# Two ways of turning the input of a superblock, and a wider gap between its load and its norm

## The chip, the cores and the metric

One core of one Trainium2 chip runs the whole kernel. The metric is the device time of one execution in microseconds (us), as the median of several runs. The profile is of one execution, which has a time of its own.

## The reference, cut to what matters

One decoder layer over a sequence of 4096 tokens of width 1024, with fp32 inputs:

```python
h = rmsnorm(x, norm_g) * (1.0 + scale) + shift      # scale, shift, gate: from c @ w_ada
proj = h @ w_in                                     # 1024 -> 3328 columns: q, k, v, gate of two head groups
y_sb = stick_breaking_attention(q, k, v) * silu(g)  # 8 heads of 64
y_sw = sliding_window_sink_attention(...) * silu(g) # 8 query heads, 2 key heads, window 128
x = x + gate * (concat(y_sb, y_sw) @ w_out)
out = rmsnorm(x, final_g)
```

Tokens are on the partitions in x; the projections need h with its 1024 features on the partitions, so every block of 128 tokens has to be turned. Each fp32 operand of a product is split into an fp16 upper half and an fp16 remainder, and a product is three passes on TensorE.

## The kernel before, in words

The sequence is cut into eight superblocks s = 0..7 of 512 tokens (`T`), each of four blocks of 128 (`NB`). `main` (L684) writes the whole order of the work into one list, `fill`, of small items with a planned cost each, and runs it from the front to the end. A superblock has 26 **units**, numbered 0 to 25 (`step`, L738): unit 0 is the key chunk of the window group, 1 to 3 three gate chunks, 4 the first query chunk; then the value units, further query and gate chunks (5 to 13); then, four times, a key, a query and a gate chunk of the stick-breaking group (14 to 25). In superblocks 1 to 7, units 5 to 9 are value units, unit 10 is the second query chunk, and behind units 10, 12 and 13 stand the output products (`o_items`, L655) of the superblock before. A chunk unit is four items of six matmuls (`part`, L398), planned at 1300 ns an item, and ends with its evacuation by ScalarE and VectorE. A query chunk's evacuation is followed by two small copies `q<-q` across partitions (L431) issued from ScalarE's queue, and the scores (`att_s1`, L516, L519, L523) need them.

Attention goes by ticks. Each pair of heads makes two groups; a group has its scores and softmax (`att_s1`), the split of its weights into two halves (`split_w`, L589, L590), the turning of these halves by DMA (`att_s2`, L595, on SyncE's queue) and the product with the values (`att_s3`, L608). A tick's due time is the planned time at the end of the pair's query unit plus `LAG` (8000 ns for the window group) plus a multiple of `TICK` (5200 ns). Ticks are written in front of the first item that is not earlier than their due time; `later(n, ...)` puts a piece of work n items later. Each engine, and each queue of DMAs, works strictly in the order written.

The input of superblock s + 1 is made ready during superblock s by `x_items` (L349), four steps for each block b: `load` (x from HBM, L318, SyncE's queue; for block 0 also the two rows of scale and shift, broadcast to all partitions, L305 and L306), `norm` (square and sum on ScalarE, L325; reciprocal root on GpSimd, L312 and L313; two items later the modulation, VectorE L365 and GpSimd L366), `split` (upper half on ScalarE L372, remainder on GpSimd L373) and `turn` (two transposing DMAs, L379). A step is placed behind the unit that `when` gives it (L731, L732):

```python
            o, e = (0, 4) if s else (9, 3)
            when = [[o + i + 3 * b for b in range(NB)] for i in (0, 1, 2, e)]
```

So for s of 1 to 6 the loads stand behind units 0, 3, 6, 9, the norms behind 1, 4, 7, 10, the splits behind 2, 5, 8, 11 and the turns behind 4, 7, 10, 13. In superblock 0 all of it stands nine units later, from 9 to 21. Superblock 7 has none of it.

Superblock 0's own input is turned at the start by fp32 transposes on TensorE (`setup_x0`, L146, L171 and L172). During superblock 0 the weights are also staged: each chunk unit loads one chunk of `w_in` (L273), splits one on ScalarE (L289) and VectorE (L290), and writes it to a scratch in HBM (L293). And `setup_wo_items` (L217) prepares the output weights in items that are strewn in by a count of the items written (`beat`, L714 to L721): every fourth one (every second one near the start). Those are eight loads, eight `gates`, then `bcast` (L239, L242, VectorE), `spread` (two fp32 products on TensorE, L247, which need bcast's result, and their evacuation) and eight `wo` (VectorE L254, ScalarE L260, GpSimd L261). Steps of `x_items` count as items too.

The tiles `f` (four buffers, in turn) hold x, the staged weights and the output rows; `hi` and `bc` have two buffers, the PSUM tiles `mm` four and `z` one.

Of the kernel before, what the change touches and what calls it, by code (L numbers as in the profile page):

```python
# [7 lines left out]
F32 = mybir.dt.float32  # L8
F16 = mybir.dt.float16
# [3 lines left out]
AF = mybir.ActivationFunctionType  # L13
ALU = mybir.AluOpType
# [3 lines left out]
D = 1024  # L18
KD = D // 128
# [3 lines left out]
T = 512  # L23
NB = T // 128
# [28 lines left out]
class Kern:  # L53
# [163 lines left out]
    def setup_wo_items(self):  # L217

        nc = self.nc
        pool = self.P["yT"].pool  # L220
        half = lambda i, name: pool.tile([128, 512], F32, tag=f"yT{i}", name=name)
        gb = [half(8 + n, "gb") for n in range(2)]
        raw = self.wo.rearrange("p m e n -> p m (e n)").bitcast(F32)
        st = {}

        def gates(k):
            ck = self.cond[:, k:k + 1]
            for n in range(2):
                t = raw[:, k, n * 512:(n + 1) * 512]
                if k == 0:  # L230
                    nc.vector.tensor_scalar(out=gb[n], in0=t, scalar1=ck, scalar2=None, op0=ALU.mult)
                else:
                    nc.vector.scalar_tensor_tensor(out=gb[n], in0=t, scalar=ck, in1=gb[n], op0=ALU.mult, op1=ALU.add)
            self.later(4, lambda: nc.sync.dma_start(out=raw[:, k], in_=self.w_out[k * 128:(k + 1) * 128, :]))

        def bcast():
            for k in range(KD):
                sl = gb[k // 4][:, (k % 4) * 128:(k % 4 + 1) * 128]
                nc.vector.scalar_tensor_tensor(out=sl, in0=self.ident, scalar=self.col[:, 32 + k:33 + k], in1=sl,  # L239
                                               op0=ALU.mult, op1=ALU.add)  # L240
            ones = st["ones"] = half(10, "onesq")[:, 0:128]
            nc.vector.memset(ones, 1.0)  # L242

        def spread():
            pss = [self.mm(), self.mm()]
            for n in range(2):
                nc.tensor.matmul(out=pss[n], lhsT=st["ones"], rhs=gb[n], start=True, stop=True)  # L247
            for n in range(2):
                nc.vector.tensor_scalar(out=gb[n], in0=pss[n], scalar1=WS, scalar2=None, op0=ALU.mult)

        def wo(m):
            t = [half(10 + n, "wot") for n in range(2)]
            for n in range(2):
                nc.vector.tensor_tensor(out=t[n], in0=raw[:, m, n * 512:(n + 1) * 512], in1=gb[n], op=ALU.mult)  # L254
            self.later(2, lambda: halves(t, m))

        def halves(t, m):
            for n in range(2):
                sl = slice(n * 512, (n + 1) * 512)
                nc.scalar.activation(self.wo[:, m, 0, sl], t[n], AF.Copy)  # L260
                nc.gpsimd.tensor_tensor(out=self.wo[:, m, 1, sl], in0=t[n], in1=self.wo[:, m, 0, sl], op=ALU.subtract)  # L261

        return [lambda k=k: self.mod_load(2, k, raw[:, k]) for k in range(KD)] + \
            [lambda k=k: gates(k) for k in range(KD)] + [bcast, spread] + [lambda m=m: wo(m) for m in range(KD)]


    def stage_load(self):
# [81 lines left out]
    def x_items(self, s, row0):  # L349

        nc = self.nc
        st = {}

        def load(b):
            if b == 0:
                self.load_mod()
            st[b] = self.x_load(self.x[bass.ds(row0 + b * 128, 128), :])

        def norm(b):
            xt = st[b]  # L360
            r = self.ssq(xt, self.hT[s][:, b, 0])
            self.later(2, lambda: modulate(xt, r))

        def modulate(xt, r):
            nc.vector.scalar_tensor_tensor(out=xt, in0=xt, scalar=r, in1=self.ab, op0=ALU.mult, op1=ALU.mult)  # L365
            nc.gpsimd.tensor_tensor(out=xt, in0=xt, in1=self.sb, op=ALU.add)  # L366

        def split(b):
            xt = st[b]
            hi = self.P["hi"].tile([128, D], F16, tag="hi", name="hi")  # L370
            lo = xt.bitcast(F16)[:, 0:D]
            nc.scalar.activation(hi, xt, AF.Copy)  # L372
            nc.gpsimd.tensor_tensor(out=lo, in0=xt, in1=hi, op=ALU.subtract)  # L373
            st[b] = (hi, lo)

        def turn(b):
            hl = st.pop(b)
            for e in range(2):
                nc.sync.dma_start_transpose(out=self.hT[s][:, b, e], in_=hl[e])  # L379

        return [[(0.0, lambda f=f, b=b: f(b)) for f in (load, norm, split, turn)] for b in range(NB)]


    def chunk_items(self, s, c, evac):
# [299 lines left out]
    def main(self):  # L684
        nc = self.nc
        NS = self.NS
# [29 lines left out]
        def add(items, after=-1):  # L716
            for ns, f in items:
                fill.append((ns, f, after))
                beat[0] += 1
                if extra and (beat[0] % 4 == 0 or 6 <= beat[0] < 20 and beat[0] % 2 == 0):  # L720
                    fill.append((0.0, extra.pop(0), -1))  # L721

        def pair_groups(s, pair):
            for g in range(2):
                self.groups.append((len(fill), s, pair, g))

        last_group = {}
        for s in range(NS):
            xi = self.x_items(s + 1, (s + 1) * T) if s + 1 < NS else []
            xat = {}  # L730
            o, e = (0, 4) if s else (9, 3)  # L731
            when = [[o + i + 3 * b for b in range(NB)] for i in (0, 1, 2, e)]  # L732
            for b, its in enumerate(xi):
                for i, it in enumerate(its):
                    xat.setdefault(when[i][b], []).append(it)
            unit = [0]

            def step(items, after=-1):  # L738
                add(items, after)
                add(xat.pop(unit[0], []))  # L740
                unit[0] += 1

            add([(0.0, lambda s=s: self.new_hT(s + 1))])
            step(self.chunk_items(s, SWK, self.evac_k(s, 4, "ksw")))
            for p in range(3):
                step(self.chunk_items(s, SWG + p, self.evac_g(s, 4 + p)))
            vi = self.v_items(s, s * NB)
            step(self.chunk_items(s, SWQ, self.evac_q(s, 4)))
            pair_groups(s, 4)
            nv = 5 if s else 3  # L750
            vo = [0, 1, 4, 2, 3]
            for i in vo[:nv]:
                step(vi[i])
            for p in range(1, 4):
                if p == 2:
                    step(self.chunk_items(s, SWG + 3, self.evac_g(s, 7)))
                step(self.chunk_items(s, SWQ + p, self.evac_q(s, 4 + p)))
                pair_groups(s, 4 + p)
                if s > 0 and p == 1:
                    add([(0.0, self.load_fg)])  # L760
                if s > 0:
                    add(self.o_block(s - 1, p - 1, (s - 1) * T), last_group[s - 1])
                elif p < 3:
                    step(vi[vo[2 + p]])
            if s > 0:
                add(self.o_block(s - 1, 3, (s - 1) * T), last_group[s - 1])
            for p in range(4):
                chunks = [self.chunk_items(s, SBK + p, self.evac_k(s, p, "ksb")),
                          self.chunk_items(s, SBQ + p, self.evac_q(s, p)),
                          self.chunk_items(s, SBG + p, self.evac_g(s, p))]  # L770
                for ch in chunks:
                    step(ch)
                pair_groups(s, p)
            assert not extra and not xat, (len(extra), xat)
            last_group[s] = len(self.groups) - 1
# [251 lines left out]
```

## Time and profile before

| | |
|---|---|
| median of 3 runs | 1802.67 us (1802.04 to 1804.15) |
| the profiled execution: its time | 1803.36 us |
| the profiled execution: span from first to last instruction | 1801.7 us |
| mean granted TensorE clock | 0.971 |
| busy: VectorE, ScalarE, GpSimd | 57%, 40%, 33% |
| TensorE's chain: share of matmul line L398 in the chain that ended last | 38% |

A busy TensorE is not one at its peak, since its clock is granted in two levels, 1.2 and 2.4 GHz (0.5 and 1.0 of full speed; a mean between them is a mixture over time). A wait is put down to the semaphore that came last.

### The profile page before, as it was taken

The page shows a single profiled execution, that of the slowest core. Times are in us where ns is not written, and L with a number is a line of the kernel's source. Part 1 is how long each engine was busy: PE and PEld are TensorE (multiplying, and loading weights), DVE is VectorE, ACT ScalarE, POOL GpSimd, SP SyncE. Part 2 cuts the span into 40 slices and gives each one's busy share as a digit, 9 for nine tenths or more (in the row PEclk, how much of TensorE's full clock was granted, in tenths as well). Part 3 has the DMA queues.
Part 4 walks back from the last instruction along what each step waited for, and adds up shares of the span by engine and source line. Part 5 has one row for each costly group of instructions (what it writes and reads, how often), then busy time and mean ns, then how long its engine had stood idle before and what let it go on. Part 6 is the DMA issues. An engine that isn't in the chain of part 4 may idle for free.

```text
span 1801.7 us, 28070 instructions
## 1 busy us (share of the span) xinstructions
PE 1676.5 (93%) x10758; PEld 859.3 (48%) x10758; DVE 1028.4 (57%) x1853; ACT 720.4 (40%) x1416; POOL 592.6 (33%) x737
## 2 busy tenths in 40 slices
PE   3797689999999999999999999999999999999987
PEld 2353334454554555544554545545555445545443
DVE  6468786455745656554654557456564556345562
ACT  3345543354334433444334534344434434244331
POOL 2015644332344323432343323343243323123231
PEclk9898889999999999999999999999999999999999
DMA  7877688475765677557674767557575567445552
GB/s 269 285 216 166 138 213 189 112 161 146 166 151 147 149 156 185 109 149 170 148 194 100 166 154 177 138 141 163 149 182 120 148 163 156 107 123 131 152 135 72
DMA packets 425859, 283.52 MB, mean 157 GB/s; under 512 B 350156, under 2 KB 376820, under 8 KB 425716
## 3 DMA queue, kind: packets, MB, share of 16 engines
q1 hardware_dynamic: 383428, 185.16, 45.2%
q10 hardware_dynamic: 42288, 96.49, 18.2%
q8 instruction: 86, 1.41, 0.3%
q14 instruction: 57, 0.47, 0.1%
HBM read 152.59 MB, written 27.80 MB: 100 GB/s over the span
## 4 chain that ended last, share of the span: by engine, by line
PE 72%; DVE 8%; DMA 6%; POOL 4%; ACT 4%; issue 3%; SPq 1%; ACTq 0%; POOLq 0%; DVEq 0%
PE mm L398 38%; PE mm L655 16%; PE mm L471 6%; PE pv L608 5%; PE z L523 4%; DMA f<-in_x_dram 3%; PE mm L483 2%; DMA q<-q 2%; ACT p L567 1%; POOL p L576 1%; DVE acc L127 1%; POOL f L366 1%; DVE w L290 1%; DMA f<-in_w_in_dram 1%; PE z L519 1%
## 5 line engine op out<-in xcount | busy, mean ns | idle before, releaser
L398 PE MATMUL mm<-hT,w 128*128 128x512 f16 x4032 | 918.9, 384 | 16.9 <-DVE w L290 8.6
L398 PEld LDWEIGHTS <-w 128*128 128x128 f16 x4032 | 389.9, 99 | 477.3 <-issue 23.4
L655 PE MATMUL mm<-wo,yT 128*128 128x512 f16 x1536 | 353.3, 386 | 0.0
L576 POOL TENSOR_SCALAR p<-p,smm 128x256 f32<-128x256 f32 x256 | 122.2, 498 | 419.6 <-DVE smm L574 360.0
L655 PEld LDWEIGHTS <-yT 128*128 128x128 f16 x1536 | 150.5, 99 | 175.8 <-issue 8.8
L626 POOL TENSOR_TENSOR yT<-gs,yT 128x256 f16<-128x256 f32 x128 | 140.0, 1093 | 240.5 <-DVE yT L625 223.2
L567 ACT ACTIVATE p<-sp,nm 128x256 f32<-128x256 f32 (+1 forms) x256 | 126.0, 493 | 204.2 <-DVE nm L560 204.0
L471 PE MATMUL mm<-wv,hT 128*128 128x512 f16 x768 | 175.2, 383 | 6.2 <-ACT wv L289 5.5
L537 DVE TENSOR_TENSOR_SCAN nb<-nb,d 128x768 f32<-128x768 f32 x64 | 115.9, 1810 | 112.1 <-ACT nb L531 112.1
L533 POOL TENSOR_SCALAR_AFFINE_SELECT beta<-beta 128x512 f32<-128x512 f32 x64 | 83.7, 1308 | 257.9 <-ACT beta L532 214.2
L590 DVE SCALAR_TENSOR_TENSOR w<-p,w 128x1024 f16<-128x1024 f32 x64 | 85.1, 1330 | 68.8 <-ACT w L589 68.8
L589 ACT ACTIVATE w<-beta 128x768 f16<-128x768 f32 x64 | 53.9, 843 | 165.4 <-DMA wT<-w 95.9
L471 PEld LDWEIGHTS <-hT 128*128 128x128 f16 x768 | 74.9, 99 | 93.0 <-issue 9.8
L560 DVE CUSTOM_DVE_ANT_0 sp<-z,bias,nsink 128x256 f32<-128x256 f32 (+1 forms) x256 | 107.2, 474 | 14.8 <-PE z L523 14.4
L608 PEld LDWEIGHTS <-v 128*64 128x64 f16 x2304 | 89.1, 110 | 55.4 <-issue 51.4
L608 PE MATMUL pv<-wT,v 128*64 128x128 f16 (+1 forms) x2304 | 110.1, 240 | 3.5 <-DVE yT L625 2.5
L531 ACT ACTIVATE nb<-z 128x768 f32<-128x768 f32 x64 | 51.7, 808 | 134.4 <-issue 58.5
L589 ACT ACTIVATE w<-p 128x1024 f16<-128x1024 f32 x64 | 67.6, 1056 | 86.8 <-POOL p L576 37.6
L366 POOL TENSOR_TENSOR f<-f,sb 128x1024 f32<-128x1024 f32 x28 | 75.5, 2695 | 44.9 <-DVE f L365 44.9
L462 DVE SCALAR_TENSOR_TENSOR v<-mm,v 128x512 f16<-128x512 f32 (+1 forms) x64 | 31.3, 489 | 94.0 <-ACT v L461 92.5
L373 POOL TENSOR_TENSOR f<-f,hi 128x1024 f16<-128x1024 f32 x28 | 61.4, 2194 | 63.5 <-ACT hi L372 63.5
L590 DVE SCALAR_TENSOR_TENSOR w<-beta,w 128x768 f16<-128x768 f32 x64 | 62.4, 976 | 34.7 <-ACT w L589 34.7
(108 smaller groups left out, 1700.6 us busy)
## 6 DMA issues: line engine op xcount, KB each, us to landing
w<-wsc ACTq DMA_DIRECT2D x147, 512.0 KB, 3.5
f<-in_x_dram SPq DMA_DIRECT2D x64, 512.0 KB, 4.2
q<-q ACTq DMA_DIRECT2D x128, 128.0 KB, 3.6
out_dram<-f SPq DMA_DIRECT2D x32, 512.0 KB, 3.9
f<-in_w_in_dram SPq DMA_DIRECT2D x26, 512.0 KB, 6.8
wo<-in_w_ada_dram SPq DMA_DIRECT2D x24, 512.0 KB, 8.1
wsc<-w SPq DMA_DIRECT2D x21, 512.0 KB, 5.1
wo<-in_w_out_dram SPq DMA_DIRECT2D x8, 512.0 KB, 5.5
```

The source lines that it names most:

```text
L366: nc.gpsimd.tensor_tensor(out=xt, in0=xt, in1=self.sb, op=ALU.add)
L398: nc.tensor.matmul(out=ps, lhsT=w[:, k, a, :], rhs=hT[:, :, b, k, :], start=(k == 0 and i == 0), stop=(k == KD - 1 and i == 2))
L471: nc.tensor.matmul(out=ps, lhsT=hT[:, tb, b, k, :], rhs=self.wv[:, k, a, 0:512], start=(k == 0 and i == 0), stop=(k == KD - 1 and i == 2))
L537: nc.vector.tensor_tensor_scan(out=nbf, data0=nbf, data1=d1, initial=1.0, op0=ALU.mult, op1=ALU.max)
L560: nc.vector.tensor_tensor_reduce(out=sp[:, u, c0:256], in0=z[:, u, c0:256], in1=bias[:, c0:256], scale=-2.0 ** -(h + 1), scalar=self.nsink ...
L567: nc.scalar.activation(p[:, u, c0:256], sp[:, u, c0:256], AF.Exp, scale=-1.0, bias=nm[:, u:u + 1], accum_out=sm[:, u:u + 1])
L576: nc.gpsimd.tensor_scalar(out=p[:, u, :], in0=p[:, u, :], scalar1=sm[:, u:u + 1], scalar2=1.0, op0=ALU.mult, op1=ALU.mult)
L589: nc.scalar.activation(hi, w, AF.Copy, scale=WS)
L590: nc.vector.scalar_tensor_tensor(out=lo, in0=w, scalar=WS, in1=hi, op0=ALU.mult, op1=ALU.subtract)
L608: nc.tensor.matmul(out=pv[h * 64:(h + 1) * 64, o0:o0 + c1 - c0], lhsT=v[:, a, vc:vc + 64], rhs=wT[:, e, h, c0:c1], start=(n == 0 and i == ...
L626: nc.gpsimd.tensor_tensor(out=y[:, 1, cols], in0=y32, in1=y[:, 0, cols], op=ALU.subtract)
L655: nc.tensor.matmul(out=ps, lhsT=y[:, a, tb * 128:(tb + 1) * 128], rhs=self.wo[:, m, b, n * 512:(n + 1) * 512], start=(m == OORD[0] and i = ...
```

## The change

Three edits. The input of superblock 1 is made ready by a new function, `x_items_pe`, on two pairs of blocks: load, norm without modulation (L328, in place), then for every two of the eight column groups of 128 four fp32 transposes on TensorE into one PSUM tile, two ScalarE passes that apply scale and shift from columns (tile `h32`, in the buffers `hi`), and for each of the two blocks a VectorE copy to fp16 and a GpSimd subtraction. Its steps stand behind units 19 to 25. For superblocks 2 to 7 the four steps stay as they are, and their places change. An empty item is put between `bcast` and `spread`.

```diff
-            [lambda k=k: gates(k) for k in range(KD)] + [bcast, spread] + [lambda m=m: wo(m) for m in range(KD)]
+            [lambda k=k: gates(k) for k in range(KD)] + [bcast, lambda: None, spread] + [lambda m=m: wo(m) for m in range(KD)]
...
+    def x_items_pe(self, s, row0):
...
+        def load(g):
+            for b in (2 * g, 2 * g + 1):
+                st[b] = self.x_load(self.x[bass.ds(row0 + b * 128, 128), :])
+
+        def norm(g):
+            for b in (2 * g, 2 * g + 1):
+                self.x_norm(st[b], self.hT[s][:, b, 0])
+
+        def tr(g, k):
+            ps = self.mm()
+            for j in range(2):
+                for i in range(2):
+                    nc.tensor.transpose(ps[:, j * 256 + i * 128: j * 256 + (i + 1) * 128],
+                                        st[2 * g + i][:, (k + j) * 128:(k + j + 1) * 128], self.ident)
+            h = self.P["hi"].tile([128, D], F16, tag="hi", name="h32").bitcast(F32).rearrange("p (j n) -> p j n", j=2)
+            for j in range(2):
+                nc.scalar.activation(h[:, j, :], ps[:, j * 256:(j + 1) * 256], AF.Identity,
+                                     bias=self.s16[:, k + j:k + j + 1], scale=self.a16[:, k + j:k + j + 1])
+            for i in range(2):
+                hT = self.hT[s][:, 2 * g + i]
+                hb = h[:, :, i * 128:(i + 1) * 128]
+                nc.vector.tensor_copy(hT[:, 0, k:k + 2, :], hb)
+                nc.gpsimd.tensor_tensor(out=hT[:, 1, k:k + 2, :], in0=hb, in1=hT[:, 0, k:k + 2, :], op=ALU.subtract)
+
+        return [[(0.0, lambda g=g: load(g)), (0.0, lambda g=g: norm(g))] +
+                [(440.0, lambda g=g, k=k: tr(g, k)) for k in range(0, KD, 2)] for g in range(2)]
...
-            xi = self.x_items(s + 1, (s + 1) * T) if s + 1 < NS else []
+            xi = [] if s + 1 == NS else (self.x_items if s else self.x_items_pe)(s + 1, (s + 1) * T)
             xat = {}
-            o, e = (0, 4) if s else (9, 3)
-            when = [[o + i + 3 * b for b in range(NB)] for i in (0, 1, 2, e)]
+            when = [[0, 2, 5, 8], [2, 4, 7, 10], [3, 5, 8, 11], [5, 7, 10, 13]]
+            if s == 0:
+                when = [[19, 22], [20, 23], [21, 24], [21, 24], [22, 25], [22, 25]]
```

For s of 1 to 6 block 0 is loaded behind the same unit and normed, split and turned one unit later; blocks 1 to 3 are loaded one unit earlier (2, 5, 8 for 3, 6, 9), and their other steps stay.

## Rows read from the trace of the kernel before

**Rows 1.** The page, part 1: busy time, share of the span, instructions.

```profile
PE 1676.5 (93%) x10758; PEld 859.3 (48%) x10758; DVE 1028.4 (57%) x1853; ACT 720.4 (40%) x1416; POOL 592.6 (33%) x737
```

**Rows 2.** Windows: superblocks 0, 1 to 6, 7, cut at unit 25's evacuation (L445).

```profile
core 0: us, PE busy (x) PEld busy (x) DVE busy (x) ACT busy (x) POOL busy (x), PEclk, DMA share, GB/s
56.00:276.31 220.31, 171.31 (x1018) 83.90 (x1016) 154.02 (x250) 104.60 (x193) 85.91 (x91) 0.88 0.77 208
276.31:1529.67 1253.36, 1227.13 (x7992) 629.31 (x7992) 704.09 (x1309) 509.19 (x1022) 431.25 (x529) 0.99 0.65 153
1529.67:1732.55 202.88, 202.88 (x1338) 104.54 (x1338) 108.67 (x216) 76.89 (x159) 49.90 (x73) 1.00 0.53 130
```

**Rows 3.** Windows: 20 us around unit 10 of superblocks 1, 6, 7; superblock 1's unit 3.

```profile
345.00:365.00 20.00, 15.86 (x89) 7.46 (x87) 6.43 (x17) 4.47 (x13) 5.12 (x8) 0.91 0.57 143
1392.00:1412.00 20.00, 16.12 (x90) 7.94 (x89) 6.25 (x16) 6.46 (x15) 5.67 (x9) 0.91 0.60 162
1597.00:1617.00 20.00, 20.00 (x120) 10.14 (x119) 7.69 (x22) 6.26 (x14) 4.12 (x7) 1.00 0.60 168
300.00:320.00 20.00, 18.46 (x140) 10.55 (x139) 8.18 (x10) 4.71 (x7) 8.74 (x8) 1.00 0.66 145
```

**Rows 4.** Timeline, superblock 2, units 8 to 10: start, length, engine, [idle before <-releaser].

```profile
538.86 16.04 SPq L595 DMA_TRANSPOSE wT<-w  x4
...
554.95 0.57 SPq L318 DMA_DIRECT2D f<-in_x_dram  x1
554.99 0.69 DVE L416 SCALAR_TENSOR_TENSOR q<-mm,q 64x512 f16<-64x512 f32 x1
...
559.16 1.06 ACT L325 ACTIVATE hT<-f 128x1024 bf16<-128x1024 f32 x1 [6.05 <-DMA f<-in_x_dram]
559.17 1.13 ACTq L431 DMA_DIRECT2D q<-q  x2
...
562.23 0.26 PE L516 MATMUL z<-kp,q 128*128 128x128 f16 x1 [3.99 <-DMA q<-q]
```

**Rows 5.** Timeline of superblock 7, unit 10, ScalarE's queue and TensorE.

```profile
1596.40 1.21 ACTq L431 DMA_DIRECT2D q<-q  x2
...
1603.22 0.27 PE L516 MATMUL z<-kp,q 128*128 128x128 f16 x2
```

**Rows 6.** Waits of TensorE from 115 to 290 us: total, times, longest.

```profile
PE z L516 <- DVE nm L560: 11.2, 2, 7.0
PE mm L398 <- DVE w L290: 8.4, 3, 6.6
PE mm L247 <- DVE onesq L242: 7.5, 1, 7.5
```

**Rows 7.** Waits of ScalarE from 115 to 280 us.

```profile
ACT hi L372 <- POOL f L366: 8.6, 3, 4.2
...
ACT hT L325 <- DMA f<-in_x_dram: 3.9, 1, 3.9
```

**Rows 8.** Window of 120 us inside superblock 0 (columns as in rows 2).

```profile
140.00:260.00 120.00, 86.08 (x502) 41.47 (x503) 93.86 (x151) 61.49 (x116) 70.55 (x69) 0.85 0.68 162
```

**Rows 9.** Groups by line: busy us, mean ns of one | idle before.

```profile
L626 POOL TENSOR_TENSOR yT<-gs,yT 128x256 f16<-128x256 f32 x128 | 140.0, 1093 | 240.5 <-DVE yT L625 223.2 <-DMA wT<-w 15.1 <-PE mm L655 2.1
...
L625 DVE CAST yT<-gs 128x256 f16<-128x256 f32 x128 | 51.6, 403 | 4.4
...
L171 PE MATMUL mm<-ident,f 128*128 128x128 f32 x32 | 5.1, 337 | 0.0
...
L172 ACT ACTIVATE xT<-mm,a 128x512 f32<-128x512 f32 x8 | 5.0, 690 | 6.3 <-PE mm L171 6.3
```

**Rows 10.** Window of the start's 32 fp32 transposes (columns as in rows 2).

```profile
26.80:32.00 5.20, 5.17 (x33) 4.93 (x33) 4.82 (x7) 3.71 (x7) 0.00 (x0) 1.00 0.61 244
```

**Rows 11.** The page, part 6: the input's transposing DMAs and their landing.

```profile
hT<-hi SPq DMA_TRANSPOSE x28, 4.5
```

**Rows 12.** Timeline at 136 us: a GpSimd addition and a VectorE cast side by side.

```profile
136.43 2.34 POOL L366 TENSOR_TENSOR f<-f,sb 128x1024 f32<-128x1024 f32 x1 [3.94 <-DVE f L365]
136.66 2.26 DVE L625 CAST yT<-gs 128x256 f16<-128x256 f32 x1
```

More of the change, by code (lines that the diff above doesn't have):

```diff
@@ L381, in x_items @@
         return [[(0.0, lambda f=f, b=b: f(b)) for f in (load, norm, split, turn)] for b in range(NB)]
+    def x_items_pe(self, s, row0):
+        nc = self.nc
+        st = {}
+        def load(g):
[21 more added lines that the diff above has]
+                [(440.0, lambda g=g, k=k: tr(g, k)) for k in range(0, KD, 2)] for g in range(2)]
     def chunk_items(self, s, c, evac):
```

## The prediction

> **What bounds the kernel now.** I read the page's busy shares first. TensorE is busy 93% of the span [rows 1], so only its idle time and its slow clock can be won. Next I cut the span into superblocks. Superblocks 1 to 6 take 1253.36 us, 208.89 each; superblock 7, the same TensorE work without the making of a next input, takes 202.88 with TensorE never idle and its clock at 1.00 [rows 2]. That is 6.01 us lost in each of six. Superblock 0 takes 220.31 us with TensorE idle for 49.0 and a clock of 0.88, though it has no output products at all [rows 2].
>
> The windows around unit 10 show where the six lose theirs: idle for 4.14 us in the first and 3.88 in the last, clock 0.91, against none and 1.00 in superblock 7 [rows 3]. The timeline of superblock 2 gives the chain. SyncE's queue holds four weight transposes L595, the last of which wait for their softmax; the load of block 3, written behind them, is issued only at 554.95 [rows 4]. ScalarE stands 6.05 us for it, up to 559.16, with the square L325. Behind that square in ScalarE's queue are the copies q<-q, issued at 559.17, though VectorE's last piece of q (L416) was done at 554.99 + 0.69 = 555.68. The scores L516 wait 3.99 us for these copies [rows 4]. In superblock 7 the copies go out 6.8 us ahead of the scores and nobody waits [rows 5].
>
> **Part 1: the steps of superblocks 2 to 7 (written in superblocks 1 to 6).** Block 3's load moves from behind unit 9 to behind unit 8. Where is that in SyncE's queue? The window pair's first tick is due 8.0 us of plan after unit 4, the split of its second group three ticks of 5.2 us later, at 23.6. Units 5 to 8 are planned at 5.2, 5.2, 5.4 (four items of 1.35) and 5.2 us, so unit 9 begins at 21.0; the split falls in its third or fourth item, and its transposes come later still. The load now stands ahead of that group's transposes, behind the first group's alone, which begin at 538.86 [rows 4], and lands long before unit 10. The square then runs as soon as ScalarE comes to it, and the copies are bound by VectorE at 555.68 instead of 559.17: 3.49 us earlier. What is late next is the same copies, now behind q itself: of the 4 us of idle time some 0.5 stays.
>
> Clock: 6.01 lost less 4.0 idle leaves 2.0 us a superblock for the slow clock. An idle time of 1.54 us left it at 1.00 in superblock 1 [rows 3], and 0.5 is nearer to that than to 4, so I take 1.8 back. Together 5.3 a superblock, **-32 us** in six. Bounds: 3.49 alone, -21; all 6.01, -36.
>
> The rest of this edit I cost at nothing. Block 0's norm, split and turn come one unit later: a unit's work covers them, and unit 0 of the next superblock, which needs the result, is 20 units away; if that cover went, the transposing DMA takes 4.5 us to land [rows 11]. Loads of blocks 1 and 2 are one unit earlier on SyncE, behind nothing new of length, and their f buffers are free by then, since the tile four places back was done a superblock earlier or in its last units.
>
> **Part 2: superblock 0.** Removed from units 9 to 21: four loads, two broadcast loads, four squares, modulations and splits, and eight transposing DMAs, which stood on SyncE ahead of staged weights and weight transposes. Moved: the steps of x no longer count as items there, so bcast, spread and the eight wo come up to three units later. Their instructions stay the same; I cost the move at nothing, as the output weights are first needed in superblock 1. The empty item makes it eight items instead of four from bcast to spread.
>
> What TensorE waited for there [rows 6], and how much I think goes:
> - spread for bcast, 7.5 us. Four more items are 5.2 us of plan: **-5.2**.
> - scores behind the softmax of the group before, 11.2. VectorE has the modulations of x among other work ahead of it; I take half, **-5.6**.
> - products behind split weights, 8.4. ScalarE, which splits them, stood 8.6 + 3.9 us for x [rows 7]; half, **-4.2**.
> - clock: 86.08 us busy at 0.85 [rows 8] are 86.08 x 0.15 = 12.9 us of lost work; a third, **-4.3**, since other waits remain.
>
> Added:
> - 32 fp32 transposes on TensorE, in units 21 to 25, where nothing covers them: the start has just 32, 5.1 us in all [rows 9], at clock 1.00 [rows 10]: **+5.1**. The Trainium skill, "TensorE: Matmul & The Clock Gate", Part 4 (PE-mode transpose), gives some 275 ns for one in a kernel; by that figure 32 would cost 8.8 us, an estimate, and the sum would be 3.7 worse. The row has 160 ns each, back to back, and decides.
> - waits for the norm ahead of each pair's first transposes. The nearest row is spread's 7.5 [rows 6]; here a whole unit lies between. 0 to 7.5 each; I take 1 each: **+2**.
> - the start of superblock 1. Behind the last eight transposes ScalarE, VectorE and GpSimd must finish before unit 0's last two items. ScalarE's passes are half the width of L172's 0.69, VectorE's copies like L625's 0.40, GpSimd's four subtractions like L626's 1.09 [rows 9]: 0.4 + 0.4 + 4.4 = 5.2, of which the three items ahead cover 3.9 of plan; with GpSimd's attention work between, **+2**; 0 to 5, were nothing covered.
>
> The copies and subtractions of earlier transposes (16 each in all) run beside chunk products. Their cover is the one to two units until superblock 1.
>
> Sum: -19.3 + 9.1 = **-10**. Bounds: all four items whole and only the transposes to pay, -40.0 + 5.1 = -35; nothing gained and all added at its worst, 5.1 + 15 + 5 = +25.
>
> **Sum.** The profiled execution took 1803.36 us; 1803.4 - 32 - 10 = 1761.4. The median lies 0.7 below that execution, so **1761 us**.
>
> **The rivals.**
> - Superblock 0 gives nothing. TensorE's waits there are waits for VectorE, busy 93.86 of 120 us [rows 8], and the new work adds to it; the stalls only move to other places. Superblock 0 then costs 0 to 25: 1771 to 1796. For it: staging and wo alone keep VectorE near its limit. Against: GpSimd and ScalarE lose all of x there, and rows 7 is standing still, not work. Chance 0.22.
> - Superblock 0 gives far more, 20 to 35, because each wait that goes lets the clock recover: 1736 to 1751. For it: 0.85 over 120 us. Chance 0.15.
> - The change doesn't do what it says: block 3's load stays behind the long wait on SyncE, because the planner puts the second group's transposes in front of unit 8's end. Then ScalarE still stands for it and only superblock 0's ten is won: about 1793. Against: the plan times above. Chance 0.06.
> - Slower. The chain TensorE, ScalarE, VectorE, GpSimd behind each of the eight groups of four transposes runs without overlap, since two hi buffers hold the results until GpSimd has read them. Per group two passes of 0.4, two copies, two subtractions of 1.09. A cast of that form took 2.26 us beside a GpSimd addition [rows 12], against 0.40 on the mean: 0.8 + 4.5 + 2.2 = 7.5, times eight 60, and 5.1: with -19.3 and -32 the time would be 1803.4 + 13.8 = 1817. It decides from 46.2 / 8 = 5.8 us a group on. The Trainium skill, "SBUF — State Buffer", Who interferes with whom, has the rule: GpSimd shares a port pair with VectorE, and whoever holds it blocks the other, copies included. The pair in rows 12 agrees with it. Against the rival: no more than two groups stand together, with a unit of 5 us or more behind them, and other work fills the waits. Chance 0.05.
>
> **How the numbers follow.** The forecast (superblock 0 between -20 and 0) has 0.52. From 1742 to 1786 it leaves out the upper part of the first rival, the lower third of the second, and the last two, 0.17 together. A measurement of this kernel can tell 0.2%, 3.6 us, from no change. Only the slower rival and the far end of the first and third could come near it: faster 0.93, within 0.2% 0.02, slower 0.05.
>
> **What would show it.** Superblocks 1 to 6: the windows around unit 10 with under 1 us idle and clock 1.00; ScalarE's wait for x gone; L516's wait for q<-q near 0.5 us each; each superblock at 203 to 204.5 us. Superblock 0: spread's wait down to about 2 us; 32 transposes of 5.1 us; superblock 1 starting about 10 us earlier, with a wait of some 2 us for hT in unit 0. Wrong would be: block 3's load still issued after the second group's transposes; waits of 5 us or more ahead of the transposes or at hT; superblock 0 as long as before.

## The result, and the profile after

The changed kernel takes 1772.36 us (median of 4 runs, 1770.9 to 1776.58) against 1802.62 beside it: a ratio of 0.9835, 95% interval [0.9816, 0.9853], some 30 us. Its profiled execution took 1770.9 us with a span of 1769.2, 32.5 less than the span of before. The time lies in the forecast range of 1742 to 1786; the forecast, 1761, was 11 us too low.

The same views as before, now of the changed kernel. Lines behind L380 have moved down by 32 (L398 is L430, L431 is L463, L516 is L548, L560 is L592); the new function's transposes are L400, its ScalarE passes L404, its casts L409 and subtractions L410. First the windows of [rows 2], cut at the same place in the work (unit 25's evacuation), with the columns of [rows 2]:

```profile
56.00:263.50 207.50, 167.11 (x1018) 85.45 (x1017) 150.67 (x263) 106.75 (x201) 84.79 (x96) 0.89 0.75 208
263.50:1498.25 1234.75, 1221.45 (x8026) 628.28 (x8027) 700.24 (x1311) 511.44 (x1024) 432.08 (x532) 1.00 0.64 155
1498.25:1701.13 202.88, 202.88 (x1338) 104.41 (x1339) 108.51 (x216) 76.83 (x159) 50.68 (x73) 1.00 0.52 129
```

Superblock 0 is 12.8 us shorter, superblocks 1 to 6 together 18.6, superblock 7 the same to the hundredth. The cut flatters superblock 0: the counts of TensorE show 34 more matmuls behind it than before (8026 against 7992). Among them are the last 8 transposes (1.1 us) and most of a group of 18 products with values (L640, 0.9 us), which the kernel before does ahead of the cut. Measured one unit later, at the evacuation of unit 0 of superblock 1, where that work is done in both, the changed kernel is at 272.76 us and the kernel before at 281.92: 9.2 us are won up to there, and the other 23 after it.

The timeline of superblock 2 around unit 10, as [rows 4]:

```profile
527.76 0.57 SPq L318 DMA_DIRECT2D f<-in_x_dram  x1
...
537.81 3.32 SPq L627 DMA_TRANSPOSE wT<-w  x2
...
539.37 1.06 ACT L325 ACTIVATE hT<-f 128x1024 bf16<-128x1024 f32 x1
...
541.18 1.56 SPq L379 DMA_TRANSPOSE hT<-hi  x1
541.22 1.19 ACTq L463 DMA_DIRECT2D q<-q  x2
542.83 1.57 SPq L379 DMA_TRANSPOSE hT<-f  x1
...
544.26 0.22 PE L548 MATMUL z<-kp,q 128*128 128x128 f16 x1
...
545.96 0.22 PE L548 MATMUL z<-kp,q 128*128 128x128 f16 x1 [1.48 <-DMA q<-q]
```

Block 3's load is issued 10 us ahead of the second group's weight transposes (537.81), and its square runs at 539.37 with no wait in front of it. But SyncE now also reaches the two transposing DMAs of block 2 (L379), which are written next, at 541.18, just as the copies q<-q go out at 541.22. The first copy lets a score begin after 3.04 us, as in [rows 4]; the second comes only after 4.74, and TensorE stands 1.48 us. In [rows 4] the same two DMAs were issued at 555.57 and 556.90 and off SyncE by 558.98, ahead of the copies at 559.17.

The waits of TensorE from 115 to 290 us, as [rows 6]:

```profile
PE mm L400 <- DVE f L330: 15.4, 4, 8.6
PE z L548 <- ACT beta L564: 4.5, 1, 4.5
PE z L548 <- DMA q<-q: 4.2, 3, 3.0
PE z L548 <- DVE nm L592: 3.6, 1, 3.6
PE mm L430 <- POOL hT L410: 0.9, 1, 0.9
PE mm L430 <- DVE hT L409: 0.3, 1, 0.3
PE mm L430 <- DVE w L290: 0.3, 1, 0.3
```

All three waits of [rows 6] have shrunk or gone: 11.2 to 3.6, 8.4 to 0.3, and spread's (L247) from 7.5 to none. In their place stands a new one of 15.4 us, the transposes' for the norm (L330). The scores of a group stand behind the softmax of the group before in more rows than that of [rows 6]; the kernel before also has these, in the same window:

```profile
PE z L516 <- ACT beta L532: 3.8, 2, 2.6
PE z L523 <- DVE nm L560: 1.7, 1, 1.7
PE z L523 <- ACT beta L532: 1.4, 1, 1.4
PE z L516 <- DMA q<-q: 0.5, 2, 0.3
```

So all waits behind softmax fall from 11.2 + 3.8 + 1.7 + 1.4 = 18.1 to 3.6 + 4.5 = 8.1 us, while those for q<-q rise from 0.5 to 4.2. The groups by line of the new work, and TensorE's timeline of the transposes:

```profile
L410 POOL TENSOR_TENSOR hT<-h,hT 128x256 f16<-128x256 f32 x16 | 13.4, 868 | 4.0 <-DVE hT L409 4.0
L409 DVE CAST hT<-h 128x256 f16<-128x256 f32 x16 | 8.1, 553 | 3.6 <-ACT h L404 3.6
L404 ACT ACTIVATE h<-mm,s,a 128x256 f32<-128x256 f32 x16 | 7.7, 561 | 6.5 <-DVE q L448 6.5
L400 PE MATMUL mm<-ident,f 128*128 128x128 f32 x32 | 6.6, 355 | 15.4 <-DVE f L330 15.4
```

```profile
223.22 0.47 PE L400 MATMUL mm<-ident,f 128*128 128x128 f32 x1 [8.64 <-DVE f L330]
223.88 1.75 PE L400 MATMUL mm<-ident,f 128*128 128x128 f32 x7 [0.19 <-DVE f L330]
...
252.09 0.45 PE L400 MATMUL mm<-ident,f 128*128 128x128 f32 x1 [5.22 <-DVE f L330]
253.83 1.76 PE L400 MATMUL mm<-ident,f 128*128 128x128 f32 x7 [1.30 <-DVE f L330]
264.18 1.09 PE L400 MATMUL mm<-ident,f 128*128 128x128 f32 x8
```

Each pair of blocks pays once, 8.64 + 0.19 and 5.22 + 1.30. The two waits have different beginnings:

```profile
215.05 4.36 POOL L261 TENSOR_TENSOR wo<-wot,wo 128x512 f16<-128x512 f32 x2 [0.69 <-DVE wot L254]
216.91 1.06 ACT L325 ACTIVATE hT<-f 128x1024 bf16<-128x1024 f32 x1
222.42 1.41 DVE L330 TENSOR_SCALAR f<-f,r 128x1024 f32<-128x1024 f32 x2
...
242.31 2.61 SPq L627 DMA_TRANSPOSE wT<-w  x2
245.02 1.02 SPq L318 DMA_DIRECT2D f<-in_x_dram  x2
249.08 1.06 ACT L325 ACTIVATE hT<-f 128x1024 bf16<-128x1024 f32 x1 [3.93 <-DMA f<-in_x_dram]
```

TensorE stands from 214.58 for the first pair. Its x was loaded long before (issued at 202.26), but ScalarE comes to the square only at 216.91, GpSimd is at the output weights (L261) until 219.41, and VectorE comes to the norm at 222.42. For the second pair TensorE stands from 246.87, and here x itself is late: its load is issued only at 245.02, behind weight transposes (L627) in SyncE's queue, and ScalarE stands 3.93 us for it. That is a hold of the same kind as the one that part 1 removes.

### The profile page after: what moved, and what is told of

The parts are those of the page before. It is cut to its first block, busy times and chain, and to the rows that moved or that the text cites. A ratio compares the mean times of both kernels' runs of the same rounds, so it can differ in the third digit from the quotient of the medians.

```text
span 1769.2 us, 28179 instructions
## 1 busy us (share of the span) xinstructions
PE 1666.3 (94%) x10790; PEld 859.7 (49%) x10790; DVE 1020.9 (58%) x1869; ACT 725.0 (41%) x1428; POOL 592.5 (33%) x745
## 4 chain that ended last, share of the span: by engine, by line
PE 74%; DVE 9%; ACT 6%; DMA 4%; POOL 3%; issue 3%; SPq 1%; ACTq 0%; POOLq 0%; DVEq 0%
PE mm L430 40%; PE mm L687 14%; PE mm L503 7%; PE pv L640 5%; PE z L555 4%; PE mm L515 2%; ACT p L599 2%; DMA q<-q 2%; DVE w L290 1%; DVE acc L127 1%; DMA f<-in_x_dram 1%; POOL p L608 1%; ACT hT L325 1%; DMA f<-in_w_in_dram 1%; DVE w L622 1%
## 5 line engine op out<-in xcount | busy, mean ns | idle before, releaser
L430 PE MATMUL mm<-hT,w 128*128 128x512 f16 x4032 | 914.2, 382 | 7.6 <-ACT w L289 2.8
L430 PEld LDWEIGHTS <-w 128*128 128x128 f16 x4032 | 389.0, 99 | 461.3 <-issue 17.6
L687 PE MATMUL mm<-wo,yT 128*128 128x512 f16 x1536 | 346.8, 381 | 0.0
L565 POOL TENSOR_SCALAR_AFFINE_SELECT beta<-beta 128x512 f32<-128x512 f32 x64 | 90.2, 1410 | 283.4 <-ACT beta L564 243.1
L503 PEld LDWEIGHTS <-hT 128*128 128x128 f16 x768 | 74.8, 98 | 93.6 <-issue 10.5
L640 PEld LDWEIGHTS <-v 128*64 128x64 f16 x2304 | 89.1, 110 | 55.3 <-issue 51.4
L592 DVE CUSTOM_DVE_ANT_0 sp<-z,bias,nsink 128x256 f32<-128x256 f32 (+1 forms) x256 | 107.2, 474 | 14.6 <-PE z L555 14.3
L640 PE MATMUL pv<-wT,v 128*64 128x128 f16 (+1 forms) x2304 | 110.1, 240 | 3.5 <-DVE yT L657 2.6
L693 DVE SCALAR_TENSOR_TENSOR f<-mm,f 128x512 f32<-128x512 f32 x64 | 43.0, 675 | 86.9 <-DMA f<-in_x_dram 70.5
L555 PEld LDWEIGHTS <-q 128*128 128x128 f16 x768 | 68.4, 100 | 20.0 <-issue 3.2
L446 DVE SCALAR_TENSOR_TENSOR q<-mm,q 64x512 f16<-64x512 f32 x64 | 43.8, 684 | 59.2 <-ACT q L445 58.6
```

The costliest lines, as they stand in the source:

```text
L430: nc.tensor.matmul(out=ps, lhsT=w[:, k, a, :], rhs=hT[:, :, b, k, :], start=(k == 0 and i == 0), stop=(k == KD - 1 and i == 2))
L503: nc.tensor.matmul(out=ps, lhsT=hT[:, tb, b, k, :], rhs=self.wv[:, k, a, 0:512], start=(k == 0 and i == 0), stop=(k == KD - 1 and i == 2))
L555: nc.tensor.matmul(out=o[:, k0:256], lhsT=q[:, j, h, cols], rhs=kt[:, kh, (qb - 1) * 128 + k0:(qb + 1) * 128], start=(j == 0), stop=(j == 1))
L592: nc.vector.tensor_tensor_reduce(out=sp[:, u, c0:256], in0=z[:, u, c0:256], in1=bias[:, c0:256], scale=-2.0 ** -(h + 1), scalar=self.nsink ...
L640: nc.tensor.matmul(out=pv[h * 64:(h + 1) * 64, o0:o0 + c1 - c0], lhsT=v[:, a, vc:vc + 64], rhs=wT[:, e, h, c0:c1], start=(n == 0 and i == ...
L687: nc.tensor.matmul(out=ps, lhsT=y[:, a, tb * 128:(tb + 1) * 128], rhs=self.wo[:, m, b, n * 512:(n + 1) * 512], start=(m == OORD[0] and i = ...
```

## The experiments

Eleven kernels ran, in three groups. The kernel before, run beside each group, took 1802.8, 1803.7 and 1803.0 us. "Unit 10" is TensorE's idle time ahead of unit 10's scores in superblocks 1 to 6, from the timeline.

| kernel | median us | ratio [95%] | unit 10, us each |
|---|---|---|---|
| before | 1802.62 | 1 | 3.88 to 4.28 |
| changed | 1772.36 | 0.9835 [0.9816, 0.9853] | 1.27 to 2.45 |
| 1 new places alone | 1775.27 | 0.9844 [0.9827, 0.986] | 1.40 to 1.66 |
| 2 transposes alone | 1795.6 | 0.9957 [0.994, 0.9973] | 3.78 to 4.45 |
| 3 empty item alone | 1802.38 | 0.9998 [0.9989, 1.0008] | 3.89 to 4.35 |
| 4 block 3's load alone | 1775.36 | 0.985 [0.9833, 0.9866] | 1.33 to 1.68 |
| 5 changed, block 2's turn later | 1757.42 | 0.9741 [0.9724, 0.9757] | 0.0 |
| 6 changed, late input by DMA | 1779.96 | 0.9863 [0.9844, 0.9882] | 1.35 to 1.64 |
| 7 changed, norm on ScalarE | 1775.4 | 0.9839 [0.9822, 0.9855] | 1.27 to 2.99 |
| 8 changed, no empty item | 1769.51 | 0.9818 [0.9799, 0.9837] | 1.30 to 1.94 |
| 9 new places, turn later, no transposes | 1766.8 | 0.9792 [0.9776, 0.9809] | 0.0 to 0.07 |
| 10 as 5, no empty item | 1757.97 | 0.974 [0.9727, 0.9754] | 0.0 to 0.2 |
| 11 as 5, norm a unit earlier | 1759.6 | 0.975 [0.9736, 0.9763] | 0.0 to 0.21 |

**1. The new places alone.** The kernel before, with the new `when` in superblocks 1 to 6:

```diff
+            if s:
+                when = [[0, 2, 5, 8], [2, 4, 7, 10], [3, 5, 8, 11], [5, 7, 10, 13]]
```

> Only the places of the steps for superblocks 2 to 7 are the new ones; superblock 0 is as before. Theory (the two parts add up, and this one ends the wait for block 3 at unit 10): superblocks 1 to 6 take about 205.8 us each as in the changed kernel, superblock 0 the old 220, so some 18.6 us less than before: 1784. Rival (the shorter superblocks come from the other way in which superblock 1's input is made): 1802.

It gave 1775.27 us, 1.56% or 28 us: most of the whole, and more than the theory's 18.6, which the windows of the changed kernel had suggested. The window of its superblocks 1 to 6:

```profile
275.58:1504.11 1228.53, 1216.89 (x7994) 625.66 (x7994) 700.49 (x1309) 509.82 (x1022) 429.35 (x529) 1.00 0.66 156
```

Superblock 0 is as it was (219.58 us against 220.31). Against [rows 2], superblocks 1 to 6 lose 24.8 us, of which idle time (window less TensorE's busy time) gives 14.6 (26.2 to 11.6) and the same matmuls at a better clock 10.2 (1227.13 to 1216.89).

**2. The transposes alone.** The changed kernel with the old places for superblocks 2 to 7:

```diff
-            when = [[0, 2, 5, 8], [2, 4, 7, 10], [3, 5, 8, 11], [5, 7, 10, 13]]
+            when = [[i + 3 * b for b in range(NB)] for i in (0, 1, 2, 4)]
```

> Only superblock 0 is new (transposes on TensorE, late places, empty item); the later steps keep their old places. Theory: superblock 0 ends 12.8 us earlier and the tail gives about 1, so 1789; ScalarE stands for block 3's load six times as before. Rival (superblock 0's gain was the scatter of one execution, or is paid back in superblock 1): 1800 or more.

It gave 1795.6 us: 0.43% less, some 7 or 8 us, between the theory's 1789 and the rival's 1800. The other part's stall is untouched (the table), and TensorE's waits show the same new one:

```profile
PE mm L400 <- DVE f L330: 15.1, 4, 7.6
```

The two parts alone add up to 28 + 8 = 36 us against 30 for both; each ratio is uncertain by about 3 us, so that is no clear conflict.

**3. The empty item alone.**

```diff
-            [bcast, spread]
+            [bcast, lambda: None, spread]
```

> The kernel before with the empty item alone. Theory A (the stall of TensorE ahead of the two products of spread, 7.5 us, is a real loss, and four more items cover it): 5 to 8 us less, 1795 to 1798. Theory B (VectorE sets the pace of superblock 0, so the stall only comes back at another place): within 2 us of before, with the waits of TensorE between 115 and 290 us still near 36 us in sum.

No difference: 0.9998 [0.9989, 1.0008], Theory B. Spread's wait falls only from 7.5 to 5.3, and that for split weights is 8.8 (8.4 in [rows 6]). Wait of TensorE from 115 to 290 us in this kernel:

```profile
PE mm L247 <- DVE onesq L242: 5.3, 1, 5.3
```

**4. Block 3's load alone.** One number of the kernel before:

```diff
+            if s:
+                when[0][3] = 8
```

> The kernel before with one step moved: block 3 of superblocks 2 to 7 is loaded behind unit 8, not 9. Theory (all of the gain of superblocks 1 to 6 hangs on this load): as much as the run with all places moved, some 18 us less, 1784. Rival (blocks 0 to 2 carry a part, by the waits of ScalarE at the norms of block 0): less than two thirds of it, 1790 or more.

1775.36 us, the same as all the moved steps of run 1 (again more than the 18 us expected). Of the new `when` nothing else shows, the second unit between load and norm of the other blocks included; and here too block 2's turn and the copies go out together, and 1.33 to 1.68 us stay.

**5. Block 2's turn later.** The changed kernel, with that turn written behind unit 10's output product:

```diff
-            when = [[0, 2, 5, 8], [2, 4, 7, 10], [3, 5, 8, 11], [5, 7, 10, 13]]
+            when = [[0, 2, 5, 8], [2, 4, 7, 10], [3, 5, 8, 11], [5, 7, 99, 13]]
...
                     add(self.o_block(s - 1, p - 1, (s - 1) * T), last_group[s - 1])
+                    add(xat.pop(99, []))
```

> The changed kernel with the two transposing DMAs of block 2 moved from behind unit 10 to behind the output product that follows it. Theory (the 1.5 us that TensorE still waits at unit 10 are the copies of q flying beside these two DMAs, 4 us and more instead of 3.06): the wait falls under 0.7 us in each of six superblocks, and with fewer falls of the clock the time is 5 to 8 us less than the changed kernel's, 1764 to 1767. Rival (the copies are late because VectorE makes q late): no difference, 1772, wait still 1.5.

1757.42 us, 15 us below the changed kernel (11.2 between the two profiled spans), more than the 5 to 8 expected. The timeline of superblock 2 in this kernel:

```profile
541.67 1.19 ACTq L463 DMA_DIRECT2D q<-q  x2
...
544.57 1.24 SPq L379 DMA_TRANSPOSE hT<-hi  x1
544.72 0.30 PE L548 MATMUL z<-kp,q 128*128 128x128 f16 x2
```

The copies fly alone, both scores begin after 3.05 us, and there is no idle time; so in all six superblocks. Windows of superblock 1, superblocks 2 to 6, and 7:

```profile
262.51:471.16 208.65, 206.02 (x1346) 106.20 (x1346) 119.17 (x223) 86.97 (x174) 75.29 (x94) 0.99 0.63 153
471.16:1490.94 1019.78, 1018.91 (x6713) 524.38 (x6714) 582.78 (x1091) 424.76 (x851) 356.81 (x440) 1.00 0.66 157
1490.94:1690.35 199.41, 199.35 (x1307) 102.46 (x1307) 108.84 (x216) 76.69 (x159) 50.38 (x73) 1.00 0.55 132
```

In superblocks 2 to 6 TensorE is idle for 0.87 us in all. (The last cut falls 31 matmuls later in the work than in the changed kernel, so superblock 7 alone is not to be compared.) Over superblocks 1 to 7 together TensorE's busy time is 1424.28 us here and 1424.33 in the changed kernel. So between these two executions the 9.8 us that this stretch is shorter are idle time, and the clock, which the expectation counted on too, gave nothing more. That the turn beside the copies made the rest of the stall is shown; in what way it delays them, no run takes apart.

**6. The old way, only later.** Superblock 1's input by the four old steps, behind units 13 to 25, with no transposes on TensorE:

```diff
-            xi = [] if s + 1 == NS else (self.x_items if s else self.x_items_pe)(s + 1, (s + 1) * T)
+            xi = [] if s + 1 == NS else self.x_items(s + 1, (s + 1) * T)
...
-                when = [[19, 22], [20, 23], [21, 24], [21, 24], [22, 25], [22, 25]]
+                when = [[13 + i + 3 * b for b in range(NB)] for i in (0, 1, 2, 3)]
```

> The changed kernel, but superblock 1's input is turned by DMA with the old steps, four units later than before the change (loads behind 13, 16, 19, 22, last turn behind 25). Theory A (superblock 0 gained because the input's work left the units 9 to 18, however it is turned): as fast as the changed kernel or faster, 1766 to 1773, with no transposes on TensorE and no wait for them. Theory B (what counts is that the turning leaves SyncE's queue and the DMA engines): no better than the kernel with the gap alone, 1775 to 1780.

1779.96 us, no better than the new places alone (1775.27) and in Theory B's range: being late by itself wins nothing. TensorE's waits from 115 to 290 us in this kernel:

```profile
PE mm L430 <- DMA hT<-hi: 13.6, 1, 13.6
PE z L548 <- ACT beta L564: 10.7, 2, 6.8
PE z L548 <- DVE nm L592: 4.9, 2, 4.3
...
PE mm L430 <- DVE w L290: 3.5, 3, 1.5
PE z L555 <- DVE nm L592: 3.1, 1, 3.1
```

The wait for split weights shrinks here too (8.4 to 3.5), and spread's is gone: for these two, moving the input's steps to later units is enough. The waits behind softmax don't shrink: 10.7 + 4.9 + 3.1 = 18.7 us here, against 18.1 before and 8.1 in the changed kernel. So in these profiles the new way buys two things over the old one moved later: these 10 us, and the start of superblock 1, which here waits 13.6 us for the last transposing DMA. Which part of the old steps' work holds the softmax up, no run takes apart.

**7. The norm's multiplication on ScalarE** (L330 was on VectorE), the same place:

```diff
-                self.x_norm(st[b], self.hT[s][:, b, 0])
+                scaled(st[b], self.ssq(st[b], self.hT[s][:, b, 0]))
+
+        def scaled(xt, r):
+            self.later(2, lambda: nc.scalar.activation(xt, xt, AF.Identity, scale=r))
```

> The changed kernel with the four multiplications by the norm (L330) on ScalarE in place of VectorE. Theory (the 15 us that TensorE waits ahead of the transposes are VectorE's queue, which is behind TensorE there): the wait falls under 6 us, and with it 5 to 9 us of time, 1763 to 1767. Rival (all engines are about as late as VectorE, the stall moves into ScalarE's queue): 1770 or more, with a wait of 10 us and more behind ScalarE.

1775.4 us, not to be told from the changed kernel, as the rival had it; the wait only changes its name (this kernel's L403 and L397 are the transposes and the multiplication):

```profile
PE mm L403 <- ACT f L397: 16.9, 4, 7.5
```

**8. The changed kernel without the empty item** (the line of run 3 taken back).

> The changed kernel without the empty item. By the run with the empty item alone it does nothing by itself: 1770 to 1775. Rival (once the input is out of the way the distance counts, and spread stalls TensorE again for 4 us and more): 1777 or more.

1769.51 us, half a us below what was expected, its interval overlapping the changed kernel's. There is no wait of spread (L247) here at all, so its going isn't the empty item's doing.

**9. No transposes, block 2's turn later.** Run 1 with run 5's move.

> The kernel before with the new places of the steps in superblocks 1 to 6, block 2's turn behind the output product, and superblock 0 as it was: against the run with block 2's turn moved (1757.42 us) it lacks only the second superblock's input by transposes on TensorE. Theory A: once the steady superblocks don't wait for q<-q, the transposes are worth what they gave alone, 7 us, up to the 12 us by which superblock 0 ended earlier: 1764 to 1769 us, superblock 0 ending at 275 to 276 us, superblock 1 about 204. Theory B: what superblock 0 wins by them is paid back in superblock 1, and they are worth the 3 us by which the whole change beat the run with the new places alone (1772.36 against 1775.27): 1759 to 1761 us.

1766.8 us, ratio 0.9792 against run 5's 0.9741: 0.0051 x 1803 = 9.2 us for the transposes. Theory A. Moving the turn gains 8.5 us without the transposes (run 1 to run 9) and 15 with them, uncertain by some 4.5 each.

**10. Run 5 without the empty item.**

> The changed kernel with block 2's turn behind the output product, and without the empty item between bcast and spread. Theory A, the empty item does nothing: 1755.5 to 1759.5 us. Theory B, it cost the 2.85 us by which the run without it was below the changed kernel (1769.51 against 1772.36): 1754 to 1755 us, with TensorE's wait for the norm L330 at about 13 us instead of 15.

1757.97 us: nothing, Theory A. The 3 us of run 8 don't come again.

**11. Run 5, each pair's load and norm one unit earlier** in superblock 0:

```diff
-                when = [[19, 22], [20, 23], [21, 24], [21, 24], [22, 25], [22, 25]]
+                when = [[18, 21], [19, 22], [21, 24], [21, 24], [22, 25], [22, 25]]
```

> The changed kernel with block 2's turn behind the output product, and in superblock 0 each pair's load and norm one unit earlier (units 18 to 22), the transposes where they were: two units instead of one lie between norm and transposes. Theory A: VectorE and ScalarE come to the norm less than a unit late, so the first transposes of a pair wait 3 us or less in all instead of 14.8 (L400 for L330), superblock 0 ends 8 to 14 us earlier, at 249 to 254 us, and the whole takes 1744 to 1750 us. Theory B: VectorE has no time to spare there, and the norm ahead of other work makes the attention's waits (L548 for L592, L564) and those for weights longer by as much: 1754 to 1760 us, superblock 0 ending at 260 us or later.

1759.6 us: Theory B. Its waits of TensorE from 115 to 290 us:

```profile
PE mm L430 <- DVE ksb L448: 9.4, 3, 4.5
...
PE mm L400 <- DVE f L330: 3.8, 3, 1.4
```

The wait for the norm falls from 14.8 us (run 5) to 3.8, and chunk products now wait 9.4 for VectorE's evacuations (L448), a wait that run 5 doesn't have: 13.2 together. All waits of this window add up to 30.5 us, and to 30.9 in run 5. So a norm one unit earlier wins nothing by itself, though it also brings the second pair's load forward (issued at 238.31, and ScalarE waits only 0.34 us for it); that the other work of these units is more than VectorE can do in time is the likely reason, argued and not shown.

## Why the prediction was right, and where 11 us went

**Part 1, the mechanism: right.** Block 3's load stood behind the long hold of SyncE; ahead of it, ScalarE's wait and the copies' delay go. Run 4 shows that this one step carries the whole part. The planner argument held too: the load is issued at 527.76, ahead of the second group's transposes, so the rival that the change doesn't do what it says falls.

**Part 1, the size: -32 forecast, -28 measured (run 1; 24.8 in superblocks 1 to 6 of the profiles).** The clock term was good: 1.8 a superblock, 10.8 in six, against 10.2. The term that was mis-sized is the wait, 3.49 a superblock or 20.9 in six: "of the 4 us of idle time some 0.5 stays". Run 1 gives 14.6 us of idle time, and 1.4 to 1.7 stays each time. The signs that the prediction named for this part, under 1 us idle at unit 10 and 203 to 204.5 us a superblock, did not come in the changed kernel (1.27 to 2.45, and 1234.75 / 6 = 205.8). The prediction asked what is late next and named the copies bound by VectorE; it did not follow SyncE's queue one step further, to block 2's turn behind the load. Freed with it, the turn meets the copies. Run 5 moves it and gets the rest; the part with this move (run 9, ratio 0.9792) is worth 37.5 us, about the prediction's bound of -36.

**Part 2: -10 forecast; -9.2 by the changed profile at unit 0 of superblock 1.** By whole runs the part is worth 7 to 8 us alone (run 2), 9.2 on clean superblocks (9 to 5), and 3 on top of run 1 (1775.27 to 1772.36); each difference of two runs is uncertain by some 4.5, so these don't differ clearly. The sum was near, by terms that were not: that is luck. Windows of the kernel before and of the changed kernel, both from 56 us to that evacuation, close the account:

```profile
56.00:281.92 225.92, 176.93 (x1052) 86.81 (x1050) 159.51 (x257) 107.45 (x198) 88.83 (x94) 0.88 0.76 207
```

```profile
56.00:272.76 216.76, 175.20 (x1080) 90.15 (x1078) 157.07 (x273) 111.43 (x210) 89.27 (x102) 0.90 0.74 205
```

Idle time falls from 49.0 to 41.6, by 7.4 us, and busy time by 1.7, though the transposes add 6.6 to it; so the products lost 8.3. Term by term:

- Removed, in the waits of TensorE from 115 to 290 us: spread's -7.5 (forecast -5.2), the softmax wait of [rows 6] -7.6 (-5.6), behind split weights -8.1 (-4.2): 23.2 for 15.0. That they went was right, why only in part: the prediction gave spread's to the empty item, and runs 3, 6 and 8 show that it went with the input's steps. In the other direction the wait for q<-q rose by 3.7, a term that the prediction doesn't have.
- The wait for the norm: 15.4 instead of +2. This is the step that failed: "here a whole unit lies between". A unit in the written order is no unit of time where ScalarE, GpSimd and VectorE are behind (the first pair), nor where the load itself is held in SyncE's queue (the second). The bound of 0 to 7.5 a pair was passed by the first pair, 8.83, and the prediction's own sign of being wrong, waits of 5 us or more ahead of the transposes, came true. On either engine (run 7) and in either place (run 11) about the same time is paid. No run moves the second pair's load alone, so what that would win is open.
- The transposes: 6.6 us instead of 5.1. By the 275 ns that the Trainium skill, "TensorE: Matmul & The Clock Gate", Part 4 (PE-mode transpose), gives for a bf16 one, they would have been 8.8, an estimate; the row gives 206 ns on the mean, between [rows 9] and that figure. The timeline shows why it isn't the 160 of [rows 9]: the first eight of each pair, behind the wait, take 2.2 us (0.47 + 1.75), and the second eight 1.09, 136 ns each. The clock tells the two apart, as windows of the changed kernel show (the first eight of either pair, then the second eight of the first):

```profile
223.20:225.70 2.50, 2.29 (x9) 1.82 (x10) 2.40 (x5) 1.17 (x2) 1.01 (x1) 0.50 0.51 151
252.00:255.60 3.60, 2.21 (x9) 1.82 (x10) 2.48 (x5) 1.99 (x4) 1.71 (x3) 0.50 0.41 141
233.80:235.00 1.20, 1.20 (x16) 1.02 (x11) 1.20 (x2) 0.92 (x2) 1.20 (x2) 1.00 0.00 0
```

  The granted clock is 0.50 (1.2 GHz) behind the waits of 8.64 and 5.22 us, and 1.00 (2.4 GHz) a unit later.
- The clock: -4.3 forecast, half of what came. The products' 8.3 us are of this kind, less what four matmuls fewer take; the granted clock of the stretch rose from 0.88 to 0.90. Behind the new waits it was down all the same, as the rows above show.
- The start of superblock 1: +2 forecast; waits of 0.9 + 0.3 for hT, and it is counted in the idle time above.

**Where the 11 us went.** Between the profiled executions 32.5 us were won where 42 were forecast. Of the missing 9.5, 8.7 lie behind the evacuation of unit 0 of superblock 1 (23.3 won for 32): most of it the waits at unit 10, which block 2's turn kept alive, 10.5 us in all where the prediction left 3. The other 0.8 are superblock 0's. The rest is the median, which lies 1.5 above the profiled execution.

**The rivals.** The time alone doesn't tell the forecast from the first rival: 1772 lies at the foot of that rival's 1771 to 1796, and only the windows and runs 2 and 9 show that superblock 0 did gain. That superblock 0 gives nothing was half right: the stalls did move, 15.4 us of them, but not all. That it gives 20 to 35 by the clock falls with the 9.2: the clock's part was 8.3. The slower rival, a serial chain behind each of eight groups, needed 5.8 us a group: the groups by line give casts of 8.1 / 8 = 1.0, subtractions of 13.4 / 8 = 1.7 and passes of 7.7 / 8 = 1.0, and the waits of TensorE for them (hT) are 1.2 in all.

## What to carry to other kernels

When a transfer that was held in an in-order queue is freed, everything written behind it is freed with it: follow that queue on to the next transfers, and ask which urgent one they will meet in flight. Here the freed turn kept a third of the stall alive, and moving one more step took the rest. Where the engines or the queue that feed a stage are behind their order, work that is added there is late by however far they are behind: count units of the order as time only where the timeline shows them keeping up, the load's queue included.

## What was unexpected of the hardware

The two copies q<-q, alone in flight, let both scores begin after 3.05 us (run 5); beside the two transposing DMAs of another queue the first score begins after 3.04 and the second after 4.74 (superblock 2 of the changed kernel). There the delay falls on the second copy alone.

The new casts L409 show a spread of four between equal instructions (minimum, median, maximum in ns, from the view of that line):

```profile
L409 DVE CAST hT<-h x16: 273/305/1221, 228.5 to 268.8; 128x256 f16<-128x256 f32 x16
```

In the timeline the short ones, 0.27 to 0.31 us, start with GpSimd free or nearly done; the long ones, 0.75 to 1.22, start inside an instruction of GpSimd and end behind it (241.21 to 242.43 beside one of GpSimd's from 240.51 to 241.82). By the rule of the Trainium skill that the prediction cited ("SBUF — State Buffer", Who interferes with whom), the second to come waits for the whole instruction of the first; these rows agree with it. Its price here is small, 16 casts of 553 ns instead of 305, some 4 us beside other work.
